# Hybrid diffusion backbone on one core: 67-row products for the grouped-query maximum, four PSUM banks for the gates' projection, rotations one block later

## The chip, the cores and the metric

One core of a Trainium2 chip runs the whole program. The metric is the device time in microseconds (us) of one execution. The engines are named as the profile names them: PE (TensorE, with PEld for its weight loads), DVE (VectorE), ACT (ScalarE), POOL (GpSimd) and SP (SyncE, which issues the DMAs).

## The reference, cut to what matters

Two layers work on 512 latent tokens and 256 context tokens of width 1024. Layer 0 joins chunked gated linear attention (GLA, four heads) with grouped-query attention (GQA, eight query heads of width 64 on two key heads). The change touches the gates of the first and the scores of the second:

```python
def gla_output(o_dirs, og, norm_g):
    o = merge_dirs(o_dirs, 2).transpose(0, 2, 1, 3)
    o = rms_norm(o, norm_g, LN_EPS) * jax.nn.silu(og.reshape(b, n, GLA_HEADS, GLA_DV))

def windowed_gqa(q, k, v, k_ctx, v_ctx, sink):
    s_loc = jnp.einsum('bnqhgd,bnkhd->bhgnqk', qb, kw).astype(F32) * scale
    s_loc = jnp.where(valid, s_loc, -jnp.inf)
    s_ctx = jnp.einsum('bnqhgd,bkhd->bhgnqk', qb, k_ctx).astype(F32) * scale
    p = jax.nn.softmax(jnp.concatenate([s_loc, s_ctx, s_sink], -1), axis=-1)

# in mixer_ab, ahead of it, for the latent tokens alone:
att_lat = windowed_gqa(axial_rope(q_l, row, col), axial_rope(k_l, row, col), v_l, k_c, v_c, sink)
```

Layer 1 (RWKV-7 and latent attention) and the two MLPs are untouched by the change.

## The kernel before, in words

All dense products take three matmuls for one (high by high, high by low, low by high part of fp32 numbers; helper `mm3`, lines 344 to 348). `weights` loads one block of 128x1024 weights by an SP DMA, ACT casts the high part (L323) and DVE subtracts the low part (L324); two buffers of each part, so the cast for block b+2 waits for the end of block b. Every engine runs its own instructions in order. That order is not the order of the source: a list scheduler works it out when the kernel is built, from priorities and its own idea of durations, and the weights of a block come with a raised priority.

The part of layer 0 that the change touches has three stretches.

**Projections and rotation (`mixer0`, the loop at L911).** Block 0 gives the GQA keys (`kg`), blocks 1 to 4 the queries (`qg`). After its 48 wide matmuls ACT moves a block out of PSUM with a factor (L916, L917), PE multiplies it by a permutation (`rp`, L919), and DVE makes the rotation from it (L921 to L923). For the keys ACT then writes the rounded keys `KS` (tile `ks`, L927), DVE the remainders `K2` (tile `k`, L928), and ACT the value one into rows 64 to 66 of `K2` (L929). Two steps of a generator that computes the modulation vectors (DMA `araw`, DVE L392) follow each block. In PSUM this stretch has six banks for products and two for the rest.

**Gates (`mixer0`, the loop at L951).** Four more blocks give the output gates `og`, evicted by ACT (L482 to L484) and DVE (L956). The pool `PB` gives six banks to products and two to tag `u`. Between the blocks runs the set-up of GLA head 0 and its first levels.

**GLA and GQA together (L984 to L989).** A generator `gla` walks over 12 windows (head by pair of chunks); beside the products of one window (`base`, `lev`, `o`) it makes the levels of the next (`lk` on POOL, `lq` on DVE, exponentials on ACT). Two of every five of its steps also advance `gqa`, and what is left of `gqa` runs alone at the end. The pool has two banks each for `b`, `u`, `q` and `qo`. `base` sums matmuls of 128, 64 and 32 columns in one bank and ends with a product of zeros (`zerob`, L655). `gqa` takes the heads in turn: while `attend(h)` runs, `scores(h + 1)` finds the maximum of each query's scores. For it POOL copies the remainders of the queries to `Q2` (tile `q`, two buffers, L737); then there are six products with the context keys (`gsc`, L745 and L746) and four with the latent keys (`gsl`, L753 to L758), each the sum of a 128-row product of `qs` and `KS` and a 64-row product of `Q2[0:64]` and `K2[0:64]`. DVE reduces them (L747, L759). Minus the maximum, in three parts, then goes to rows 64 to 66 of `Q2` (L776), and `attend` uses 67 rows of `Q2` and `K2` (L800, L811), so that the maximum is taken off inside the product. Its masks (L798) and those of the scores (L756) are bf16 products of 128 rows.

Of the kernel before, what the change touches and what calls it, by code (L numbers as in the profile page):

```python
# [7 lines left out]
F32 = mybir.dt.float32  # L8
# [19 lines left out]
PF = dict(b=6, n=2)  # L28
PM = dict(b=4, s=2)
PZ = dict(b=4, n=2, m=2)  # L30
PB = dict(b=6, u=2)
SG = 3
PG = 2, 2, 2, 2
PS = 3, 2, 3
# [223 lines left out]
class Build:  # L258
# [453 lines left out]
    def gqa(self, m0, mx_, queries, KS, K2, vg, hi, lo):  # L712
# [20 lines left out]
        def scores(h):  # L733
            kv, qs = h // 4, QS[h]
            q2[h] = Q2 = m0.tile([99, T], F32R, name="q2", bufs=2)
            for t0, n in PARTS:
                nc.gpsimd.tensor_copy(Q2[0:64, t0:t0 + n], qs[HALF[h % 2], t0:t0 + n])  # L737
            yield
            mx = m0.tile([P, 2, 6], F32, name="mx", bufs=2)
            blk = lambda n: slice(n * P, n * P + P)  # L740
            for i in range(3):
                b = self.bank("gsc", "q").rearrange("p (a k) -> p a k", a=2)
                for a in range(2):
                    q = blk(2 * i + a)
                    mm(b[:, a], qs[:, q], KS[kv][:, CX], start=True, stop=False)  # L745
                    mm(b[:, a], Q2[0:64, q], K2[kv][0:64, CX], start=False, stop=True)  # L746
                nc.vector.tensor_reduce(mx[:, 0, 2 * i:2 * i + 2], b, axis=AX.X, op=ALU.max)  # L747
                yield
            for n in range(4):
                j0, j1 = max(n - 1, 0), min(n + 2, 4)  # L750
                ks = slice(j0 * P, j1 * P)
                b = self.bank("gsl", "q")[:, 0:(j1 - j0) * P]
                mm(b, qs[:, blk(n)], KS[kv][:, ks], start=True, stop=False)  # L753
                for j in (n - 1, n + 1):
                    if 0 <= j < 4:
                        mm(b[:, (j - j0) * P:(j - j0 + 1) * P], self.identb, self.maskb[0 if j < n else 1],  # L756
                           start=False, stop=False)
                mm(b, Q2[0:64, blk(n)], K2[kv][0:64, ks], start=False, stop=True)  # L758
                nc.vector.tensor_reduce(mx[:, 1, n:n + 1], b, axis=AX.X, op=ALU.max)  # L759
                if n % 2:  # L760
                    yield
            ne = m0.tile([P, 6, 2], F32, name="ne", bufs=2)
            nc.vector.tensor_tensor(mx[:, 0, 0:4], mx[:, 0, 0:4], mx[:, 1, 0:4], op=ALU.max)
            nc.vector.tensor_scalar(ne[:, :, 0], mx[:, 0], self.c('sink', h), -1.0, op0=ALU.max, op1=ALU.mult)
            nc.scalar.activation(ne[:, :, 1], ne[:, :, 0], AF.Exp, bias=self.c('sink', h))
            me = mE[h % 2]
            nc.vector.tensor_copy(me[:, :, 0::32], ne)
            nc.vector.tensor_tensor(ne, ne, me[:, :, 0::32], op=ALU.subtract)
            nc.vector.tensor_copy(me[:, :, 1::32], ne)
            nc.vector.tensor_tensor(me[:, :, 2::32], ne, me[:, :, 1::32], op=ALU.subtract)  # L770
            yield
            for t0, n in PARTS:
                b = self.bank("mrow", "q")
                for a in range(n // P):
                    mm(b[0:35, a * P:a * P + P], me[:, t0 // P + a], self.identb, start=True, stop=True)
                nc.scalar.copy(Q2[64:99, t0:t0 + n], b[0:35, :n])  # L776
            yield
# [74 lines left out]
    def mixer0(self):  # L852
# [3 lines left out]
        with tc.tile_pool(name="m0", bufs=1, side="right", reuse_waits="tile") as m0, ExitStack() as m0_, \  # L856
# [25 lines left out]
            with tc.tile_pool(name="ma", bufs=1, reuse_waits="tile") as ma:  # L882
                self.load(ma, 'rope')
                for w in range(2):
                    nc.sync.dma_start(self.sd[w:w + 1], self.scb[0:1, w])

                def mods():
                    for l, j in ((0, 2), (0, 4), (0, 3)):
                        yield from self.ada_chunk(ma, l, j)
                gen = mods()  # L890
                step = lambda n: [next(gen, None) for _ in range(n)]
                nc.vector.memset(a1T, 0.0)

                for t in range(TT):
                    ps = self.bank("a1t", "n")
                    nc.tensor.transpose(ps[0:48, 0:P], at[:, t], ident)
                    nc.scalar.copy(a1T[0:16, t * P:(t + 1) * P], ps[0:16, 0:P])
                    nc.scalar.copy(a1T[32:48, t * P + 1:(t + 1) * P + 1], ps[32:48, 0:P])
                step(3)
                for b in range(4):  # L900
                    w = self.weights(self.a['w0_s'][b].rearrange("p k m -> p (k m)"))
                    for (t0, n), o in zip(PARTS, self.dense(*w, hi, lo, KT)):
                        for hh in range(2):
                            for r in HALF:
                                if b < 2:
                                    nc.scalar.mul(qd[b * 2 + hh][r, t0:t0 + n], o[HALF[hh]], 0.125)
                                else:
                                    nc.scalar.copy(kd[b * 2 - 4 + hh][r, t0:t0 + n], o[HALF[hh]])
                    step(2)

                for b in range(5):  # L911
                    w = self.weights(self.a['w0_s'][4 + b].rearrange("p k m -> p (k m)"))
                    ol, oc = self.dense(*w, hi, lo, KT)
                    x = ma.tile([P, T], F32, name="kg") if b == 0 else qg[b - 1]
                    sc = 1.0 if b == 0 else 0.125
                    nc.scalar.mul(x[:, 0:NL], ol, sc)  # L916
                    nc.scalar.mul(x[:, NL:T], oc, sc)  # L917
                    rp = self.bank("rp", "n")
                    nc.tensor.matmul(rp, self.kr('rperm'), x[:, 0:NL], start=True, stop=True)  # L919
                    rt = ma.tile([P, NL], F32, name="ropet", bufs=2)  # L920
                    nc.vector.tensor_tensor(rt, rp, self.kr('sin'), op=ALU.mult)  # L921
                    nc.vector.tensor_tensor(x[:, 0:NL], x[:, 0:NL], self.kr('cos'), op=ALU.mult)
                    nc.vector.tensor_tensor(x[:, 0:NL], x[:, 0:NL], rt, op=ALU.add)  # L923
                    if b == 0:
                        for i in range(2):
                            for r in HALF:
                                nc.scalar.copy(KS[i][r], x[HALF[i]])  # L927
                            nc.vector.tensor_tensor(K2[i][0:64], x[HALF[i]], KS[i][HALF[i]].bitcast(F32), op=ALU.subtract)  # L928
                            nc.scalar.activation(K2[i][64:67], x[64:67], AF.Identity, scale=0.0, bias=self.c('one')[64:67])  # L929
                    step(2)  # L930
                self.proj_moving(1, hi, lo, ev1)
                step(3)
                for _ in gen:
                    pass
# [27 lines left out]
            mhi, mlo = self.act_tiles()  # L962
            self.psum(PG[0], u=PG[1], q=PG[2], qo=PG[3])
            with tc.tile_pool(name="mb", bufs=1, reuse_waits="tile") as mb:
                self.zerob = mb.tile([32, P], BF16, name="zerob")
                nc.gpsimd.memset(self.zerob, 0.0)
                self.identb = mb.tile([P, P], BF16, name="identb")
                nc.gpsimd.tensor_copy(self.identb, ident)
                self.maskb = [mb.tile([P, P], BF16, name=f"maskb{i}") for i in range(2)]
                mt = m1.tile([P, 2 * P], F32, tag="Dt", name="mt", bufs=4)  # L970
                nc.sync.dma_start(mt, self.a['band'])
                for i in range(2):
                    nc.gpsimd.tensor_copy(self.maskb[i], mt[:, i * P:(i + 1) * P])
                self.gla_setup(mb)

                def queries(i):

                    for r, o, a in ((HALF[0], HALF[1], mhi.k(4 + i)), (HALF[1], HALF[0], mlo.k(4 + i))):
                        for t0, n in PARTS:
                            sl = slice(t0, t0 + n)  # L980
                            nc.scalar.copy(a[r, sl], qg[i][r, sl])
                            nc.vector.tensor_tensor(a[o, sl], qg[i][r, sl], a[r, sl].bitcast(F32), op=ALU.subtract)
                    return mhi.k(4 + i), mlo.k(4 + i)
                att = self.gqa(mb, m0, queries, KS, K2, vg, mhi, mlo)  # L984
                for i, _ in enumerate(self.gla(mb, setup, g, qd, kd, og, mhi, mlo)):
                    if i % 5 < 2:
                        next(att, None)
                for _ in att:
                    pass  # L989
# [1047 lines left out]
```

## Time and profile before

| | us |
|---|---|
| median of 3 runs (2107.3 to 2122.47) | 2110.19 |
| the profiled execution, its own time | 2109.45 |
| its span | 2107.6 |
| PE busy | 1979.7 (94%) |
| DVE busy | 1346.8 (64%) |
| ACT busy | 949.2 (45%) |
| POOL busy | 306.7 (15%) |

Times in the rows are microseconds from the start of the span, durations of one instruction in a group are nanoseconds where the group says so. A matmul's duration is its latency: matmuls overlap, so the distance from one start to the next tells what one costs. The releaser that a row names is the event that came last; where a wait is for several engines it can be another.

### The profile page before, as it was taken

The page shows a single profiled execution, that of the slowest core. Times are in us where ns is not written, and L with a number is a line of the kernel's source. Part 1 is how long each engine was busy: PE and PEld are TensorE (multiplying, and loading weights), DVE is VectorE, ACT ScalarE, POOL GpSimd, SP SyncE. Part 2 cuts the span into 40 slices and gives each one's busy share as a digit, 9 for nine tenths or more (in the row PEclk, how much of TensorE's full clock was granted, in tenths as well). Part 3 has the DMA queues.
Part 4 walks back from the last instruction along what each step waited for, and adds up shares of the span by engine and source line. Part 5 has one row for each costly group of instructions (what it writes and reads, how often), then busy time and mean ns, then how long its engine had stood idle before and what let it go on. Part 6 is the DMA issues. An engine that isn't in the chain of part 4 may idle for free.

```text
span 2107.6 us, 35444 instructions
## 1 busy us (share of the span) xinstructions
PE 1979.7 (94%) x14256; PEld 1636.2 (78%) x14256; DVE 1346.8 (64%) x2471; ACT 949.2 (45%) x1829; POOL 306.7 (15%) x515
## 2 busy tenths in 40 slices
PE   7998999989899999999989999988888899999997
PEld 6877666667788888888877777667677797888887
DVE  8775898737897556534485554568887555444454
ACT  5526676544622222222255646755654544333332
POOL 0003455301200000000021020123342011000001
PEclk9999799999999999999999999988999999999999
DMA  8650000053354555323243100000001412333341
GB/s 294 204 163 14 1 2 1 1 180 103 117 180 136 156 159 148 115 58 98 82 150 120 38 11 13 11 9 2 3 2 33 135 57 86 110 99 90 90 135 41
DMA packets 67049, 181.69 MB, mean 86 GB/s; under 512 B 7490, under 2 KB 12354, under 8 KB 66756
## 3 DMA queue, kind: packets, MB, share of 16 engines
q1 hardware_dynamic: 66884, 179.42, 27.4%
q8 instruction: 112, 1.84, 0.4%
q14 instruction: 53, 0.43, 0.1%
HBM read 172.83 MB, written 5.51 MB: 85 GB/s over the span
## 4 chain that ended last, share of the span: by engine, by line
PE 75%; DVE 14%; ACT 5%; issue 3%; DMA 2%; POOL 1%; DVEq 0%; SPq 0%; ACTq 0%; POOLq 0%
PE mm L346 18%; PE mm L348 18%; PE mm L344 17%; PE var L1054 2%; PE ms L1446 2%; PE go L787 2%; PE gab L1602 1%; PE mo L1472 1%; DMA araw<-in_ada_r_dram 1%; DVE wlo L324 1%; PE lev L661 1%; DVE z L1070 1%; DVE xtmp L1657 1%; DVE X L1660 1%; PE st L1486 1%
## 5 line engine op out<-in xcount | busy, mean ns | idle before, releaser
L323 ACT CAST whi<-wraw 128x1024 fp32r<-128x1024 f32 (+2 forms) x253 | 221.5, 879 | 645.6 <-PE mm L346 559.8
L344 PE MATMUL mm<-acthi,whi 128*128 128x512 f32 (+1 forms) x1464 | 443.6, 349 | 12.3 <-ACT whi L323 11.6
L348 PE MATMUL mm<-acthi,wlo 128*128 128x512 f32 (+1 forms) x1464 | 440.0, 347 | 9.6 <-DVE wlo L324 9.4
L346 PE MATMUL mm<-actlo,whi 128*128 128x512 f32 (+1 forms) x1464 | 442.8, 348 | 2.1 <-POOL actlo L1086 2.0
L324 DVE TENSOR_TENSOR wlo<-wraw,whi 128x1024 fp32r<-128x1024 f32 (+2 forms) x253 | 256.6, 1017 | 221.0 <-ACT whi L323 216.3
L344 PEld LDWEIGHTS mm<-acthi,whi 128*128 128x128 f32 x1464 | 251.4, 192 | 50.7 <-ACT whi L323 14.2
L348 PEld LDWEIGHTS mm<-acthi,wlo 128*128 128x128 f32 x1464 | 252.1, 192 | 49.6 <-DVE wlo L324 13.5
L346 PEld LDWEIGHTS mm<-actlo,whi 128*128 128x128 f32 x1464 | 251.2, 191 | 39.1 <-issue 3.4
L348 PE MATMUL mm<-hh,wlo 128*128 128x512 f32 (+1 forms) x832 | 252.8, 341 | 3.6 <-DVE wlo L324 3.6
L344 PE MATMUL mm<-hh,whi 128*128 128x512 f32 (+1 forms) x832 | 253.8, 343 | 0.2 <-ACT hh L323 0.2
L346 PE MATMUL mm<-hl,whi 128*128 128x512 f32 (+1 forms) x832 | 253.3, 342 | 0.1
L1086 POOL TENSOR_TENSOR actlo<-lnu,acthi 128x256 fp32r<-128x256 f32 (+1 forms) x48 | 60.0, 1265 | 717.7 <-DVE lnu L1084 631.7
L348 PEld LDWEIGHTS mm<-hh,wlo 128*128 128x128 f32 x832 | 143.9, 189 | 23.3 <-DVE wlo L324 4.2
L344 PEld LDWEIGHTS mm<-hh,whi 128*128 128x128 f32 x832 | 143.1, 189 | 20.0 <-issue 1.0
L346 PEld LDWEIGHTS mm<-hl,whi 128*128 128x128 f32 x832 | 143.5, 189 | 19.2 <-issue 0.7
L1158 DVE SCALAR_TENSOR_TENSOR z<-mm,mod,z 128x512 f32<-128x512 f32 (+1 forms) x144 | 94.1, 659 | 95.9 <-PE mm L348 95.7
L392 DVE SCALAR_TENSOR_TENSOR araw<-araw,scb 128x1024 f32<-128x1024 f32 x80 | 97.8, 1223 | 53.8 <-DMA araw<-in_ada_r_dram 52.9
L1012 DVE SCALAR_TENSOR_TENSOR z<-mm,mod,z 128x256 f32<-128x256 f32 (+1 forms) x64 | 34.9, 548 | 79.7 <-PE mm L348 79.2
L323 ACT CAST hh<-relu 128x512 fp32r<-128x512 f32 (+1 forms) x100 | 50.5, 534 | 77.8 <-DVE relu L1110 77.8
L616 POOL TENSOR_TENSOR lk<-kd,Dt 64x128 f32<-64x128 f32 x144 | 74.6, 518 | 48.1 <-ACT Dt L598 19.4
L324 DVE TENSOR_TENSOR hl<-relu,hh 128x512 fp32r<-128x512 f32 (+1 forms) x100 | 56.1, 588 | 26.5 <-ACT hh L323 26.1
L392 DVE SCALAR_TENSOR_TENSOR aprod<-araw,scb 128x1024 bf16<-128x1024 f32 x48 | 58.6, 1222 | 22.4 <-DMA araw<-in_ada_r_dram 22.1
(459 smaller groups left out, 3306.5 us busy)
## 6 DMA issues: line engine op xcount, KB each, us to landing
araw<-in_ada_r_dram SPq DMA_DIRECT2D x80, 512.0 KB, 3.8
wraw<-in_w_dram SPq DMA_DIRECT2D x72, 512.0 KB, 3.6
wraw<-in_w_dram SPq DMA_DIRECT2D x144, 256.0 KB, 2.7
wraw<-in_w_s_dram SPq DMA_DIRECT2D x31, 512.0 KB, 3.7
wraw<-in_w_o_dram SPq DMA_DIRECT2D x22, 512.0 KB, 3.9
scraw<-in_ada_sc_dram SPq DMA_DIRECT2D x8, 512.0 KB, 5.8
shraw<-in_ada_sh_dram SPq DMA_DIRECT2D x8, 512.0 KB, 5.8
x<-in_xT_dram SPq DMA_DIRECT2D x8, 384.0 KB, 5.5
```

The lines of the kernel that those rows point to most:

```text
L323: self.nc.scalar.copy(hi, raw)
L324: (eng or self.nc.vector).tensor_tensor(lo, raw, hi.bitcast(F32), op=ALU.subtract)
L344: mm(o, whi, ahi[:, sl], start=first, stop=False)
L346: mm(o, whi, alo[:, sl], start=False, stop=False)
L348: mm(o, wlo, ahi[:, sl], start=False, stop=last)
L392: self.nc.vector.scalar_tensor_tensor(pr, raw, 1.0, self.scb[:, w], op0=ALU.mult, op1=ALU.mult, accum_out=out(w))
L616: nc.gpsimd.tensor_tensor(K[r, :, x], kk[r, :, x], d[r, :, x], op=ALU.mult)
L787: mm(o, vals(j), p, start=st, stop=False)
L1054: nc.tensor.matmul(var, self.c('o1024', 0, P), sq, start=(k == 0), stop=(k == KT - 1))
L1086: eng.tensor_tensor(lo[:, k, sl], u, hi[:, k, sl].bitcast(F32), op=ALU.subtract)
L1158: nc.vector.scalar_tensor_tensor(z[:, d, sl], o, self.mod[:, l, self.wh(i, parts), 5, d:d + 1], z[:, d, sl], op0=ALU.mult, op1=ALU.add)
L1446: mm(s_[:, j], a[:, c], b[:, j * 384:j * 384 + 384], start=st, stop=sp_)
```

## The change

Three edits. The pool for the gates gets four product banks in place of six. In `scores` the first three spare rows of `Q2` are set to zero by POOL ahead of the copies, and the products of the maximum take all 67 rows of `Q2` and `K2`: the three rows of ones meet three of zeros. `zerob` grows from 32 to 128 rows, so that the product that ends `base` takes 128 rows. In the projections a function `rotate` holds what followed the eviction, and is called for block b-1 after the eviction of block b, and once more after the loop.

```diff
-PB = dict(b=6, u=2)
+PB = dict(b=4, u=2)
...
             q2[h] = Q2 = m0.tile([99, T], F32R, name="q2", bufs=2)
+
+            nc.gpsimd.memset(Q2[64:67].bitcast(F32), 0.0)
             for t0, n in PARTS:
                 nc.gpsimd.tensor_copy(Q2[0:64, t0:t0 + n], qs[HALF[h % 2], t0:t0 + n])
...
-                    mm(b[:, a], Q2[0:64, q], K2[kv][0:64, CX], start=False, stop=True)
+                    mm(b[:, a], Q2[0:67, q], K2[kv][:, CX], start=False, stop=True)
...
-                mm(b, Q2[0:64, blk(n)], K2[kv][0:64, ks], start=False, stop=True)
+                mm(b, Q2[0:67, blk(n)], K2[kv][:, ks], start=False, stop=True)
...
-                for b in range(5):
-                    w = self.weights(self.a['w0_s'][4 + b].rearrange("p k m -> p (k m)"))
-                    ol, oc = self.dense(*w, hi, lo, KT)
-                    x = ma.tile([P, T], F32, name="kg") if b == 0 else qg[b - 1]
-                    sc = 1.0 if b == 0 else 0.125
-                    nc.scalar.mul(x[:, 0:NL], ol, sc)
-                    nc.scalar.mul(x[:, NL:T], oc, sc)
+                def rotate(b, x):
                     rp = self.bank("rp", "n")
...
+                late = None
+                for b in range(5):
+                    w = self.weights(self.a['w0_s'][4 + b].rearrange("p k m -> p (k m)"))
+                    ol, oc = self.dense(*w, hi, lo, KT)
+                    x = ma.tile([P, T], F32, name="kg") if b == 0 else qg[b - 1]
+                    sc = 1.0 if b == 0 else 0.125
+                    nc.scalar.mul(x[:, 0:NL], ol, sc)
+                    nc.scalar.mul(x[:, NL:T], oc, sc)
+                    if late:
+                        rotate(*late)
+                    late = b, x
                     step(2)
+                rotate(*late)
                 self.proj_moving(1, hi, lo, ev1)
...
-                self.zerob = mb.tile([32, P], BF16, name="zerob")
+                self.zerob = mb.tile([P, P], BF16, name="zerob")
```

## Rows read from the trace of the kernel before

**Rows 1.** Busy time by stretch, GLA and GQA: engines, granted clock, DMA.

```profile
200.00:242.00 42.00, 31.34 (x135) 21.42 (x134) 35.58 (x82) 28.31 (x75) 23.97 (x52) 0.59 0.01 4
242.00:270.00 28.00, 27.88 (x173) 18.90 (x172) 22.27 (x71) 18.31 (x56) 12.92 (x28) 1.00 0.01 1
270.00:310.00 40.00, 38.80 (x254) 26.98 (x254) 38.38 (x101) 29.74 (x87) 23.29 (x43) 1.00 0.01 1
310.00:340.00 30.00, 28.28 (x170) 19.31 (x168) 26.97 (x76) 20.31 (x58) 17.71 (x33) 0.94 0.00 1
340.00:400.00 60.00, 59.56 (x391) 41.75 (x390) 49.14 (x140) 37.63 (x124) 34.07 (x65) 1.00 0.00 1
400.00:437.00 37.00, 34.88 (x197) 23.14 (x195) 17.15 (x50) 17.00 (x39) 0.99 (x3) 1.00 0.00 1
```

**Rows 2.** Order of time on PE: 64-row products of `gsc`, and 67-row products of `gst`.

```profile
251.99 0.38 PE L746 MATMUL gsc<-k,q 64*128 64x256 f32 x1
...
252.61 0.38 PE L746 MATMUL gsc<-k,q 64*128 64x256 f32 x1
...
265.62 0.29 PE L811 MATMUL gst<-q,k 67*128 67x256 f32 x1
...
265.87 0.29 PE L811 MATMUL gst<-q,k 67*128 67x256 f32 x1
```

**Rows 3.** Order of time on PE: after a mask, 67 rows, and 64 rows.

```profile
257.96 0.23 PE L798 MATMUL gst<-maskb,identb 128*128 128x128 bf16 x1
258.00 0.36 PE L800 MATMUL gst<-q,k 67*128 67x256 f32 x1
258.19 0.81 PE L787 MATMUL go<-gp,vg 128*128 128x384 f32 x2
...
258.96 0.23 PE L756 MATMUL gsl<-maskb,identb 128*128 128x128 bf16 x1
259.12 0.38 PE L758 MATMUL gsl<-k,q 64*128 64x256 f32 x1
259.43 0.49 PE L651 MATMUL base<-lq,lk 128*128 128x128 f32 x2
```

**Rows 4.** Groups on POOL from 205 to 440 us (busy us, mean ns).

```profile
L494 POOL MEMSET lk<- 128x256 f32 x7 | 2.0, 302 | 0.0
...
L563 POOL MEMSET S<- 64x128 f32 x6 | 1.2, 205 | 6.0 <-PE o L646 5.9
```

**Rows 5.** Order of time on all engines, around the first query block.

```profile
106.17 1.70 ACT L927 CAST ks<-kg 64x768 fp32r<-64x768 f32 x2 [8.20 <-DVE kg L923]
...
112.55 0.60 ACT L916 ACTIVATE qg<-mm 128x512 f32<-128x512 f32 x1
...
113.19 2.07 PE L919 MATMUL rp<-qg,rope 128*128 128x512 f32 x2 [4.60 <-ACT qg L916]
```

**Rows 6.** Busy time by stretch, behind that wait and up to the end of the loop.

```profile
113.20:117.80 4.60, 4.60 (x11) 3.18 (x12) 3.26 (x7) 0.22 (x1) 0.00 (x0) 0.50 0.66 191
...
120.00:145.00 25.00, 25.00 (x136) 20.62 (x135) 22.09 (x39) 4.89 (x9) 0.00 (x0) 1.00 0.60 167
```

**Rows 7.** Order of time on all engines: evictions of the gates, and what follows.

```profile
185.95 1.14 DVE L956 SCALAR_TENSOR_TENSOR og<-mm,col,og 128x512 f32<-128x512 f32 x2 [0.36 <-ACT og L484]
...
191.11 0.88 ACT L482 ACTIVATE og<-mm 128x512 f32<-128x512 f32 x2 [0.39 <-PE mm L348]
...
193.55 1.14 DVE L956 SCALAR_TENSOR_TENSOR og<-mm,col,og 128x512 f32<-128x512 f32 x2 [1.21 <-ACT og L484]
...
207.35 1.14 DVE L956 SCALAR_TENSOR_TENSOR og<-mm,col,og 128x512 f32<-128x512 f32 x2
...
208.24 0.77 PE L651 MATMUL base<-lq,lk 128*128 128x128 f32 x2 [5.97 <-POOL mE L723]
```

**Rows 8.** A short wait of PE in order of time.

```profile
335.23 0.38 PE L745 MATMUL gsc<-ks,acthi 128*128 128x256 f32 x1 [1.01 <-ACT gp L802]
```

**Rows 9.** Busy time of the two microseconds in which the clock falls after it.

```profile
336.00:338.00 2.00, 2.00 (x5) 1.06 (x5) 2.00 (x5) 1.49 (x4) 1.45 (x2) 0.59 0.03 8
```

## The prediction, made before the change was run

> **What bounds the kernel now.** I read the slices of the page first: PE is busy nearly all the time, so only what takes PE's time, or makes it wait, can move the end. Then the busy time by stretch for the stage that the change touches, then the order of time inside it. From 242 to 437 us PE is the bound, but not alone. DVE leaves idle only 28 - 22.27 = 5.7 us from 242 to 270, 40 - 38.38 = 1.6 us from 270 to 310, 3.0 us from 310 to 340, 10.9 us from 340 to 400 and 19.9 us behind 400, where only attention is left [rows 1]. From 200 to 242 the mean granted clock is 0.59, and DVE is idle for 6.4 us of 42 [rows 1]: there PE is slow and DVE nearly full. What an edit saves on PE counts up to what DVE has idle in the same stretch.
>
> **67 rows in place of 64.** It is a PE edit whose price shows in the distance between starts. A pair of 256-column products of 128 and 64 rows repeats every 252.61 - 251.99 = 0.62 us; the same pair with 67 rows in `attend` every 265.87 - 265.62 = 0.25 us [rows 2]. That is 0.37 us for a 64-row product in a run of pairs. After a mask, the 64-row product and its neighbours take 259.43 - 258.96 = 0.47 us from the mask's start to the next start, the 67-row one 258.19 - 257.96 = 0.23 us, so 0.24 us [rows 3]. PE seems to run empty on the way into the smaller shape and out of it; 67 rows are counted as the full shape. Eight heads have six `gsc` products each, in twos, where the first change of shape costs as little as behind a mask: I take 0.33 us of 0.24 to 0.37, so 48 x 0.33 = 15.8 us. The four `gsl` of each head give 32 x 0.24 = 7.7 us. The 24 `zerob` products (12 windows of two chunks) change shape too, but the products ahead of them have 64 and 32 columns, so one change stays: between 0 and 0.24, I take 0.1 us, so 2.4 us. The sum is 26 us of PE time. One head of eight falls before 242 us, so 23 us lie between 242 and 437, or 0.118 us for each microsecond.
>
> Spread evenly, that is 3.3, 4.7, 3.5, 7.1 and 4.4 us for the five stretches. DVE's idle time caps the second at 1.6 and the third at 3.0, which leaves 19.4 us. Not all of that comes through: DVE would be full to 90% or more up to 400 us, and each engine would more often find its input late. I take 0.6 of it, 12 us; ends 6 us (a third) and 23 us (no cap).
>
> The edit adds eight POOL memsets of 3 rows by 768 elements. 256 elements take 302 ns and 128 take 205 ns [rows 4]; on that line 768 take 0.69 us, together 5.5 us. POOL is busy 34.07 of 60 us and less elsewhere [rows 1], and the memset waits for the same buffer as the copies behind it. Behind it on POOL stand those copies and the `lk` products of the next GLA window, made one window ahead; their cover is POOL's idle time. I take nothing; without the cover 5.5 us. The three more rows of the moving and loaded operands cost nothing that rows 2 would not hold. The copy of the maxima into the same rows gets a further writer to wait for, but it already waits for products that come later.
>
> **Rotations a block later.** The keys' rotation is late on DVE, ACT stands 8.20 us for it, then makes `KS` and the ones, and so moves the first query block out of PSUM only at 112.55; its rotation product on PE waits 4.60 us for that [rows 5]. Behind the wait PE runs 4.60 us at a granted clock of 0.50, the 1.2 GHz level [rows 6], so half of it, 2.3 us, is lost besides. Together 6.9 us at one place; I found no other wait of PE of such a kind in the loop. With the edit the query block's eviction comes ahead of the keys' copies on ACT, and PE takes up the rotation of a block one block of products later, when its input is long there. Moved with the matmul are three DVE operations of each block, and the keys' four ACT copies, two ACT fills and two DVE subtractions. Next late could be the cast of the weights two blocks on, behind those copies on ACT, or DVE: it is busy 22.09 of 25 us after the stall [rows 6], and the 6.9 us in which it could catch up are gone. The generator's DMAs keep their place in the source behind each block, on SP's queue. I take 6 us, ends 1 and 7.
>
> **Four banks for the gates.** It seems a loss: products can run one block less ahead. But a block needs two banks, and with four the fourth block needs those of the second, which DVE has emptied by 185.95 + 1.14 = 187.1, while the third block ends only about 191.1, where ACT begins on it [rows 7]. So 4 us cover it; the third block by the same pattern has more. If the cover went, PE would wait for the rest. What it gives is at the end. The first `base` of GLA starts at 208.24, and the row names POOL, with 5.97 us of waiting; but that memset has no part in `base`, and DVE's first eviction of the last gate block (207.35, two in 1.14 us) ends just before [rows 7]. I read it as a wait for the bank: with six banks four blocks wrap around to the first two, and the next pool's `b` is laid on these. With four, these hold the third block, emptied from 193.55 on [rows 7]. So `base` can begin 6 us earlier, on the heels of the last gate block, and PE may keep its clock. In exchange the bank of `z` (tag `u`) then comes under the last block. But DVE has only 6.4 us idle up to 242. I take 4 us, ends 0 and 6.
>
> **Sum.** 12 + 6 + 4 = 22 us. The profiled execution took 2109.45 us, 0.7 us under the median of the runs, which is nothing here. 2109.45 - 22 = 2087.5 us, 1.1% below the median.
>
> **Rivals.** First, DVE takes nearly all: it is the bound in the stage by then, 4 us come from the 67 rows (the tail alone), 1 us from the banks, 6 us from the rotation: 2109.45 - 11 = 2098.5. For it speak the 38.38 of 40 us [rows 1]; against it, that DVE's idle time also lies before 270 and behind 340.
>
> Second, rows don't count, and the 0.62 us of rows 2 come from something else in `gsc`, such as its operands: then only 6 + 4 us come, 2099.5 us. Rows 3 speak against it, where neighbours differ and the gap is still there. The Trainium skill has both sides. "TensorE: Matmul & The Clock Gate", in "Why this matters for your kernels", says that a single product of 32 rows takes as long as one of 128, and by that the 67 rows would give nothing; "TensorEngine Tiling (Array Packing)", under "Key Properties", says that a change of the tiling mode drains the engine, and by that the sum above stands. The trace agrees with the second.
>
> Third, and slower: the clock. PE fell to 0.59 in the two microseconds after a wait of only 1.01 us [rows 8, 9], with DVE the bound there. A faster PE waits more between 270 and 340, where DVE is full. PE has 38.80 + 28.28 = 67.1 us busy there [rows 1], less 8.2 saved 58.9; all at the lower level they need 117.8 us in place of 70, 48 us more. With the other gains, 22 less 0.6 x 4.6, that gives 2109.45 + 48 - 19 = 2138 us. It turns the result from where about half of these 70 us run at 1.2 GHz: 58.9 x 1.5 - 70 = 18 us, which eats the 19. Against it: waits of that length are rare now, and a slow PE soon catches up with DVE's queue and stops waiting.
>
> **How the numbers follow.** My forecast (all three act, in the sizes above) has 0.62, DVE takes nearly all 0.20, rows don't count 0.08, the clock 0.10. The forecast's own ends are 2109.45 - 23 - 7 - 6 = 2073 and 2109.45 - 6 - 1 = 2102; the order on every engine is worked out anew, which can add or take some microseconds on both sides. The range that holds 8 in 10 reaches from 2068 to 2105 and takes in the first two rivals. A measurement tells about 1% from no change, 21 us, so the line lies at 2089, just above the forecast: of the 0.62, I give 0.48 to below it (it has more room below, if the clock holds from 202 us on), and 0.02 of the rivals; slower by over 1% is most of the clock rival, 0.08; the rest 0.42.
>
> **What would show it.** Pairs of `gsc` 0.25 us apart, and `zerob` followed at once; no `rp` that waits for `qg`, and no stretch at 0.50 behind it; the first `base` at the heels of the last gate block (its distance from there, not the absolute time); from 270 to 340 DVE at 95% or more, with the waits of PE now for DVE's tiles. Wrong I would be if the early stretch keeps the full clock and its queues close up (a larger gain), if the recomputed order puts the keys' copies ahead of a weight cast and PE waits there, or if DVE's 1.6 us of idle time from 270 to 310 hold the whole stage back.

## The result, and the profile after

The changed kernel takes 2087.05 us (median of 4 runs, 2082.48 to 2089.79) beside 2111.19 us for the kernel before on the same chip (4 runs, 2107.3 to 2122.47). The ratio is 0.9884, 95% interval 0.9859 to 0.9909: 1.2% faster. 2087.5 us was predicted. The profiled execution took 2088.43 us, with a span of 2086.6 us against 2107.6 us. The total fits; its terms do not all fit, and the experiments below are about these.

All line numbers in this part are those of the changed kernel, unless the kernel before is named.

**Rotations.** Order of time on PE at the first query block, which stood still for 4.60 us before [rows 5]:

```profile
113.39 0.51 PE L348 MATMUL mm<-acthi,wlo 128*128 128x512 f32 x2
113.74 1.02 PE L915 MATMUL rp<-qg,rope 128*128 128x512 f32 x2
114.20 0.92 PE L344 MATMUL mm<-acthi,whi 128*128 128x512 f32 x2
```

Busy time by stretch around it, and up to the end of the loop:

```profile
105.00:120.00 15.00, 15.00 (x82) 12.45 (x82) 13.10 (x25) 6.86 (x10) 0.00 (x0) 1.00 0.54 164
120.00:145.00 25.00, 25.00 (x141) 21.72 (x140) 23.66 (x40) 5.20 (x10) 0.00 (x0) 1.00 0.58 173
```

`rp` carries no wait in square brackets any more (2.94 to 4.85 us in the six traces without this edit), and the stretch at 0.50 [rows 6] is gone. The first of the last gate block's two evictions on ACT starts at 199.24 us, in the kernel before at 204.64: 5.4 us earlier. Forecast: 6. (Executions of kernels that don't differ up to that place differ there by up to 2 us.)

**Four banks.** Order of time on PE at the start of GLA:

```profile
196.29 0.51 PE L348 MATMUL mm<-acthi,wlo 128*128 128x512 f32 x2
196.64 0.39 PE L651 MATMUL base<-lq,lk 128*128 128x128 f32 x2
...
199.16 0.23 PE L655 MATMUL base<-zerob 128*128 128x128 bf16 x1 [1.67 <-POOL zerob L974]
202.91 2.93 PE L508 MATMUL z<-a1T,con 48*128 48x512 f32 x4 [3.52 <-DVE og L964]
206.52 0.58 PE L747 MATMUL gsc<-ks,acthi 128*128 128x256 f32 x1 [0.69 <-DVE acthi L990]
208.04 0.58 PE L748 MATMUL gsc<-k,q 67*128 67x256 f32 x1 [0.94 <-POOL q L739]
```

`base` starts at the heels of the last gate block, as forecast, and its wait of 5.97 us [rows 7] is gone. But the four waits behind it add up to 1.67 + 3.52 + 0.69 + 0.94 = 6.82 us. The first product of `ms` (L674), the end of the first window, starts 6.2 us earlier, of which 5.4 were there before GLA began; first the changed kernel, then the kernel before:

```profile
227.14 1.22 PE L674 MATMUL ms<-sq,con 128*128 128x256 f32 x2 [0.54 <-ACT sq L672]
```

```profile
233.35 1.22 PE L674 MATMUL ms<-sq,con 128*128 128x256 f32 x2 [0.35 <-ACT sq L672]
```

The other 0.8 us are not the banks' alone, for the first head's 67-row products lie in them too. From that eviction on ACT to `ms` it is 27.90 us here, 28.71 in the kernel before, and 28.16 in the run below that has the rows and six banks: about 0.3 us for the banks. Forecast: 4. And the banks cost something at another place, the first block of the gates, where PE didn't wait before:

```profile
158.78 0.39 PE L344 MATMUL mm<-acthi,whi 128*128 128x256 f32 x1 [1.25 <-ACT vt L880]
```

This wait of 1.25 us, for the eviction of the projection ahead of the gates (`vt`), stands in the traces of all five versions with four banks and in none of the nine with six.

**67 rows.** Order of time on PE in a run of pairs, which took 0.62 us a pair before [rows 2], and the chain of one chunk's small products:

```profile
246.37 0.28 PE L748 MATMUL gsc<-k,q 67*128 67x256 f32 x1
246.49 0.28 PE L747 MATMUL gsc<-ks,actlo 128*128 128x256 f32 x1
246.60 0.28 PE L748 MATMUL gsc<-k,q 67*128 67x256 f32 x1
246.72 0.39 PE L651 MATMUL base<-lq,lk 128*128 128x128 f32 x2
247.04 0.53 PE L654 MATMUL base<-lq,lk 128*64 128x64 f32 x12
247.50 0.23 PE L655 MATMUL base<-zerob 128*128 128x128 bf16 x1
247.57 1.11 PE L661 MATMUL lev<-lq,lk 128*128 128x128 f32 x8
```

A pair now repeats every 246.60 - 246.37 = 0.23 us, and `zerob` is followed after 0.07 us. Busy time in three stretches that hold about the same work as 242 to 270, 270 to 340 and 340 to 437 us before [rows 1] (VectorE executes 72, 173 and 190 instructions in them, before 71, 177 and 190, as the rows count them):

```profile
235.00:260.00 25.00, 24.31 (x172) 17.56 (x171) 23.25 (x72) 18.73 (x57) 14.13 (x30) 1.00 0.00 1
260.00:326.00 66.00, 60.57 (x425) 43.98 (x426) 64.50 (x173) 50.27 (x145) 41.51 (x76) 0.97 0.01 1
326.00:413.00 87.00, 82.00 (x583) 60.59 (x583) 66.29 (x190) 54.11 (x160) 37.74 (x71) 1.00 0.00 1
```

The stretch as a whole has shrunk from 195 to 178 us. VectorE's work in it is the same, 23.25 + 64.50 + 66.29 = 154.0 us (before 153.9, from [rows 1]); PE's busy time fell from 189.4 to 166.9, by 22.5 us. So 17 of the 22.5 us taken from PE came out at the end. The last products of the attention (`goc`) start 24.1 us earlier; first the changed kernel, then the kernel before:

```profile
415.83 1.13 PE L789 MATMUL goc<-gp,vg 128*128 128x256 f32 x4
```

```profile
439.97 1.13 PE L787 MATMUL goc<-gp,vg 128*128 128x256 f32 x4
```

24.1 less the 6.2 above are 17.9 us for the rows behind the first window. Forecast: 12.

**What is late now.** One of the ten-microsecond stretches of 260 to 340 us, in each of which VectorE is busy for 95% or more, and the wait of PE that stands in it:

```profile
320.00:330.00 10.00, 8.33 (x54) 6.63 (x55) 9.94 (x20) 8.46 (x24) 7.66 (x11) 0.83 0.00 0
```

```profile
321.67 0.39 PE L747 MATMUL gsc<-ks,acthi 128*128 128x256 f32 x1 [1.93 <-ACT gp L804]
```

This is the wait of [rows 8], grown from 1.01 to 1.93 us, with the fall of the clock behind it [rows 9]. The memsets on GpSimd, one group:

```profile
L737 POOL MEMSET q<- x8: 732/732/732, 203.4 to 386.3; 3x768 f32 x8
```

They take 0.73 us each (estimate: 0.69), and nothing is recorded as waiting for them directly. But the first one, at 203.4, stands on POOL ahead of the `lk` products, and VectorE's wait for these has grown; first the changed kernel, then the kernel before:

```profile
205.19 0.43 DVE L597 TENSOR_TENSOR Dt<-ld 128x256 f32<-128x256 f32 x1 [1.94 <-POOL lk L616]
```

```profile
209.15 0.43 DVE L597 TENSOR_TENSOR Dt<-ld 128x256 f32<-128x256 f32 x1 [0.66 <-POOL lk L616]
```

With the rows and their memsets alone this wait is 1.54 us, with the rotations alone 0.65.

Behind the attention the stages are the same in both kernels, and the lead shrinks from 24.1 to 21.0 us at the end of the span. Such differences come between executions of one kernel: the runs above spread over 7 and 15 us.

### The profile page after: what moved, and what is told of

Read it like the earlier page. It is cut to its first block, busy times and chain, and to the rows that moved or that the text cites. A ratio compares the mean times of both kernels' runs of the same rounds, so it can differ in the third digit from the quotient of the medians.

```text
span 2086.6 us, 35456 instructions
## 1 busy us (share of the span) xinstructions
PE 1951.6 (94%) x14256; PEld 1626.4 (78%) x14256; DVE 1345.9 (64%) x2471; ACT 950.4 (46%) x1829; POOL 312.9 (15%) x523
## 4 chain that ended last, share of the span: by engine, by line
PE 72%; DVE 17%; ACT 5%; issue 3%; DMA 2%; SPq 0%; POOL 0%; DVEq 0%; ACTq 0%; POOLq 0%
PE mm L346 18%; PE mm L348 18%; PE mm L344 18%; PE var L1062 2%; PE ms L1454 2%; PE mo L1480 1%; PE gab L1610 1%; DVE z L1078 1%; DVE xtmp L1665 1%; DVE X L1668 1%; DMA araw<-in_ada_r_dram 1%; PE go L789 1%; DVE wlo L324 1%; PE st L1494 1%; DVE R L1780 1%
## 5 line engine op out<-in xcount | busy, mean ns | idle before, releaser
L324 DVE TENSOR_TENSOR wlo<-wraw,whi 128x1024 fp32r<-128x1024 f32 (+2 forms) x253 | 257.2, 1020 | 215.1 <-ACT whi L323 210.6
L324 DVE TENSOR_TENSOR hl<-relu,hh 128x512 fp32r<-128x512 f32 (+1 forms) x100 | 56.2, 588 | 26.6 <-ACT hh L323 26.2
```

What stands on the lines that cost most here:

```text
L324: (eng or self.nc.vector).tensor_tensor(lo, raw, hi.bitcast(F32), op=ALU.subtract)
```

## Experiments

The kernel before ran beside each group of four: 2112.22 us for the first, 2113.44 for the second, 2111.69 for the third. All ratios are to it, with 95% intervals.

### One edit at a time

**The 67-row products and the memset alone.**

```
+nc.gpsimd.memset(Q2[64:67].bitcast(F32), 0.0)
...
-mm(b[:, a], Q2[0:64, q], K2[kv][0:64, CX], start=False, stop=True)
+mm(b[:, a], Q2[0:67, q], K2[kv][:, CX], start=False, stop=True)
...
-mm(b, Q2[0:64, blk(n)], K2[kv][0:64, ks], start=False, stop=True)
+mm(b, Q2[0:67, blk(n)], K2[kv][:, ks], start=False, stop=True)
```

> The kernel before with the 67-row products and their memset alone (zerob, banks and rotation as before). Theory (each 64-row product makes PE change shape twice): the stretch of GLA and GQA gets shorter by 15 to 17 us, pairs of gsc follow each other 0.25 us apart, the first base still waits until the last gate eviction, so a time of about 2094. Rival (rows don't count): below 3 us, 2107 or more. Rival (DVE holds the stage): 4 to 8 us, 2102 to 2106.

2089.7 us, ratio 0.9896 (0.9863 to 0.9928): 22.0 us. The rows are nearly the whole result, and more than the 12 us that I gave them in the prediction and the 15 to 17 us ahead of this run. But for the eight memsets every engine executes the instructions of the kernel before in the same order, so a new order is not what gained them.

**The rotations alone.** The loop of the change with `rotate` and `late`, everything else as before.

> The kernel before with the rotations a block later alone. Theory: the 4.6 us wait of PE and the half-speed stretch behind it are gone, and the gates' evictions come 5.4 us earlier, as in the changed kernel; all of it reaches the end: about 2105. Rival (the later stage has slack for it, because DVE bounds it): 0 to 2 us, 2108 or more.

2105.92 us, ratio 0.9973 (0.9955 to 0.9991): 5.7 us (1.9 to 9.5), and the wait of `rp` is gone. As forecast. In exchange a projection behind the loop (`mv`, L474) waits 1.02 us for weights from DVE (`wlo`, L324).

**Four banks alone.**

```
-PB = dict(b=6, u=2)
+PB = dict(b=4, u=2)
```

> The kernel before with four banks for the gates alone. Theory after the result: the first base starts 6 us earlier, but z takes over the wait for the last gate eviction, so 0 to 1 us: about 2110. Rival (as predicted): 4 us, 2106. Rival (gates run into each other): slower by 1 us or more, with PE waiting for og in the gates.

2117.96 us, ratio 1.0023 (1.0005 to 1.0041): no gain, a small loss. Its waits of PE from 190 to 240 us, totals by line:

```profile
PE o L645 <- DVE A L663: 4.3, 1, 4.3
PE z L508 <- DVE og L956: 3.3, 1, 3.3
PE base L655 <- POOL zerob L966: 1.7, 1, 1.7
PE gsc L746 <- POOL q L737: 1.1, 1, 1.1
```

The wait of 5.97 us [rows 7] comes back as 3.3 + 1.7 + 1.1 = 6.1 us, and the 1.25 us for `vt` at the start of the gates are added. The order is that of the kernel before on every engine. The rest of the loss goes together with a lower clock: the mean granted clock of the span is 0.9598 over these 12 executions and 0.9626 over the 29 of the kernel before beside them. Within these 29 an execution is about 1.7 us longer for each 0.001 less (a straight line through them), so 0.0028 go with about 4.6 us (estimate). Why the clock is lower, no run shows.

**128 zero rows alone.**

```
-self.zerob = mb.tile([32, P], BF16, name="zerob")
+self.zerob = mb.tile([P, P], BF16, name="zerob")
```

> The kernel before with zerob of 128 rows alone. Theory: 24 products, 0.1 us each at most, 0 to 2.4 us: about 2109. Rival (both changes of shape count): 4 to 6 us, 2105.

2113.44 us, ratio 1.0002 (0.9983 to 1.0022): nothing that can be measured. On PE the step is there: from the start of L654 to the start of `lev` one chunk takes 256.14 - 255.61 = 0.53 us, in the kernel before 256.84 - 256.22 = 0.62 us, so 0.09 us for each of 24, about the 0.1 that I took.

The four parts sum to -22.0 - 5.7 + 4.9 + 0.4 = -22.4 us beside the change's -24.1 (medians); they add up within the intervals.

### Is it the switch between row counts, or the 64 rows?

In the kernel before, the two 64-row products of a pair of blocks stand side by side: 128, 64, 64, 128 rows.

```
-mm(b[:, a], qs[:, q], KS[kv][:, CX], start=True, stop=False)
-mm(b[:, a], Q2[0:64, q], K2[kv][0:64, CX], start=False, stop=True)
+ops = ((qs[:, q], KS[kv][:, CX]), (Q2[0:64, q], K2[kv][0:64, CX]))
+for s, (x, y) in enumerate(ops[::-1] if a else ops):
+    mm(b[:, a], x, y, start=s == 0, stop=s == 1)
```

> The kernel before with the two 64-row products of a pair of query blocks side by side (128, 64, 64, 128 rows in place of 128, 64, 128, 64): as many products of 64 rows as before, half as many switches between row counts. Theory (it is the switch that costs, not the 64 rows): the second 64-row product starts 0.12 us behind the first, the pair takes 0.3 us less, 24 pairs save 8 us of TensorE and 4 to 7 us of time: 2104 to 2107 us. Rival (a product of 64 rows is slow in itself): nothing is saved, 2110 to 2113 us.

2106.45 us, ratio 0.9965 (0.9948 to 0.9982): 7.4 us gained, with as many 64-row products as before. Order of time on PE:

```profile
250.46 0.36 PE L747 MATMUL gsc<-ks,actlo 128*128 128x256 f32 x1
250.75 0.50 PE L747 MATMUL gsc<-k,q 64*128 64x256 f32 x2
251.18 0.39 PE L747 MATMUL gsc<-ks,actlo 128*128 128x256 f32 x1
251.41 0.34 PE L795 MATMUL gst<-acthi,ks 128*128 128x384 f32 x1
```

Four products take 251.41 - 250.46 = 0.95 us here, 2 x 0.62 = 1.24 us in the kernel before [rows 2] and 2 x 0.23 = 0.46 us with 67 rows. One island of 64-row products costs (1.24 - 0.46) / 2 = 0.39 us over full shape; doubling its size adds only 0.95 - 0.46 - 0.39 = 0.10 us. So it is the switch that costs, by this trace. The Trainium skill, "TensorEngine Tiling (Array Packing)", "Key Properties", says that a change of the tiling mode drains the engine; the trace agrees and gives 0.39 us as the price of going there and back.

### Why four banks gave so little

**Six banks in the changed kernel** (`PB` back to `b=6`), with the same order of instructions on every engine:

> The changed kernel with six banks for the gates' projection as before: the other three edits stay. The order of instructions on every engine is that of the changed kernel. Theory (the step forecast at 4 us gained under 1 us, because the product of z then waits for the last gate's eviction in place of base): base waits 5 to 6 us again, z waits for nothing, and the time is 2086 to 2089 us, 0 to 2 us over the changed kernel. Rival A (four banks are worth what was forecast when the other edits stand beside them): 2090 to 2092 us. Rival B (they cost in company too, as they cost alone): 2081 to 2084 us.

2085.43 us, ratio 0.9870 (0.9842 to 0.9898), beside 0.9884 for the change. `base` waits again, those of `z`, `zerob` and `gsc` are gone, and so is the one for `vt` (waits of PE from 190 to 240 us):

```profile
PE o L645 <- DVE A L663: 7.1, 1, 7.1
PE base L651 <- DVE og L964: 6.2, 1, 6.2
```

**A bank of its own for the last gate block**: the products of this block get a tag with two banks, so neither `base` nor `z` lies under it.

```
-PB = dict(b=4, u=2)
+PB = dict(b=4, u=2, x=2)
...
-for (t0, n), o in zip(PARTS, self.dense(*w, hi, lo, KT)):
+for (t0, n), o in zip(PARTS, self.dense(*w, hi, lo, KT, tag="x" if b == 3 else "b")):
```

> The changed kernel with the last gate block's product in two banks of its own beside the four, so that neither base nor z comes under a bank that this block still holds. Theory (VectorE and GpSimd are full from the last gate block on, so a product that starts sooner only waits elsewhere): the wait of z of 3.5 us goes, the wait for the zeroed rows or for the half query takes over within 10 us, and the time is 2085 to 2087.5 us, at most 2 us below the changed kernel. Rival (the moved wait of z is what ate the forecast gain): the first maskings start 3 to 4 us earlier and the time is 2083 to 2084 us.

2089.94 us, ratio 0.9892 (0.9872 to 0.9911): nothing gained. The order is again the same, and the wait for `vt` is still there. Waits of PE in the same stretch:

```profile
PE o L645 <- DVE A L663: 6.9, 1, 6.9
PE gsc L747 <- DVE acthi L990: 5.5, 1, 5.5
PE base L655 <- POOL zerob L974: 1.6, 1, 1.6
PE gsc L748 <- POOL q L739: 0.9, 1, 0.9
```

What none of the three moves is the work of the other engines. Order of time on VectorE, the last eviction of the gates and the first selection of the levels, first in the changed kernel, then with six banks, then with the bank of its own:

```profile
202.10 1.14 DVE L964 SCALAR_TENSOR_TENSOR og<-mm,col,og 128x512 f32<-128x512 f32 x2
...
212.21 0.96 DVE L663 COPY_PREDICATED A<-con,lev 128x128 f32<-128x128 uint32 x3
```

```profile
203.67 1.14 DVE L964 SCALAR_TENSOR_TENSOR og<-mm,col,og 128x512 f32<-128x512 f32 x2
...
213.76 0.96 DVE L663 COPY_PREDICATED A<-con,lev 128x128 f32<-128x128 uint32 x3
```

```profile
205.07 1.14 DVE L964 SCALAR_TENSOR_TENSOR og<-mm,col,og 128x512 f32<-128x512 f32 x2
...
215.16 0.96 DVE L663 COPY_PREDICATED A<-con,lev 128x128 f32<-128x128 uint32 x3
```

The distance is 10.11, 10.09 and 10.09 us, whether `base` starts 5.46 us ahead of that eviction (196.64), 5.39 us ahead (199.68) or 0.89 us behind it (204.56). Between the two VectorE waits once for GpSimd (the 1.94 us above; 1.93 in each of the two other kernels) and then works off its queue without a pause, through the first selection, which carries no wait, to the end of the window. Busy time of that stretch in the changed kernel, and the wait of PE for the selections that come last in it:

```profile
205.19:228.40 23.21, 12.40 (x62) 9.26 (x60) 22.62 (x51) 14.78 (x39) 13.69 (x25) 0.65 0.00 1
```

```profile
224.28 0.80 PE L645 MATMUL o<-A,vt 128*128 128x128 f32 x2 [8.30 <-DVE A L663]
```

VectorE is busy 22.62 of 23.21 us. ACT is full too up to the first selection (8.77 of the 8.90 us from the last eviction's end to it, in all three kernels), but later stands 6.39 us for VectorE. The queue of VectorE has the same length behind the last gate block's eviction in all three, and doesn't ask when `base` started. A product that starts earlier only waits longer for a selection: 8.3 us in the changed kernel, 7.1 with six banks. No run here shortens this queue, so that it decides is read from the traces and not tested by an edit.

### More of the same: the other narrow products

The selection of the sink takes 99 rows, 96 of them zero, instead of 3, and `z` takes 128 rows instead of 48.

```
-sl = sel[sink, 64 - 64 * par:192 - 64 * par]
-mm(ob, sl, Q2[sink, 0:NL], start=False, stop=True)
+sl = sel[:, 64 - 64 * par:192 - 64 * par]
+mm(ob, sl, Q2[:, 0:NL], start=False, stop=True)
...
```

> The changed kernel with the remaining narrow products of this stage made full: the selection of the sink takes 99 rows (96 of them zero) instead of 3, and z takes 128 rows instead of 48. Theory (each switch of TensorE to fewer rows and back costs 0.2 to 0.33 us, and VectorE sets the pace for about half of the stage): 16 selections and 8 products of z, about 24 switches by 0.28 us are 6.7 us of TensorE, of which 2 to 5 us show: 2082 to 2085 us. Rival (the selections stand in time that VectorE sets, or 3 rows at the far end of the array switch at no cost): 2086 to 2088 us.

2089.81 us, ratio 0.9887 (0.9866 to 0.9907): nothing, where I expected 2 to 5 us. PE does save: from the products of `U` ahead of one selection to the `lev` behind it 283.00 - 281.59 = 1.41 us became 1.13. But the stage does not get shorter in the profiled execution, the longest of six (2084.82 to 2092.57 us). Busy time of the stretch that corresponds to 235 to 413 us of the changed kernel:

```profile
239.00:419.00 180.00, 164.29 (x1163) 123.84 (x1162) 153.40 (x427) 121.02 (x355) 92.33 (x173) 0.96 0.00 1
```

PE is busy 2.6 us less (166.9), idle 15.7 us instead of 11.1, and the mean clock is 0.96 instead of 0.99. What was true of the first 22.5 us is not seen for the next; whether for want of idle time on VectorE or for the clock of this execution, the run doesn't tell.

### Does VectorE set the pace?

The reduction of `gsl` is taken twice, once in the changed kernel and once in the kernel before; this adds 32 instructions of 0.48 us, 15.4 us by their durations. VectorE's busy time over the whole span rises less, by 10.1 us in the changed kernel (1345.9 to 1356.0) and by 6.4 in the kernel before (1346.8 to 1353.2).

```
-nc.vector.tensor_reduce(mx[:, 1, n:n + 1], b, axis=AX.X, op=ALU.max)
+for _ in range(2): nc.vector.tensor_reduce(mx[:, 1, n:n + 1], b, axis=AX.X, op=ALU.max)
```

> The changed kernel with the second maximum of each head (the reduction of gsl on VectorE) taken twice, with the same result: 32 instructions of 0.48 us more, 15.4 us of VectorE and nothing else. Theory (the saved time of TensorE has made VectorE the bound of the stretch, 24 us of idle time left in 178): most of it shows, 9 to 15 us, so 2096 to 2102 us. Rival (TensorE still sets the pace there): 2 to 6 us, 2089 to 2093 us.

> The kernel before with the same reduction taken twice, 15.4 us more of VectorE. Theory (VectorE has 41 us of idle time in 195 there and TensorE sets the pace): 2 to 8 us show, 2113 to 2119 us, clearly less than the same edit costs in the changed kernel. Rival (VectorE was the bound already, and the rows gained in another way): 10 to 15 us, 2121 to 2126 us.

In the changed kernel 2105.61 us, ratio 0.9968 (0.9949 to 0.9988): 18 us more than the change, by the ratios, and above the 2096 to 2102 us expected. In the kernel before 2125.65 us, ratio 1.0081 (1.0055 to 1.0108): 17 us more. My theory wanted a clearly smaller loss in the kernel before and fell on that; the time lies in the rival's range. Both losses are larger than what VectorE's busy time rose by. The order of the stage is worked out anew in both, which is part of the price. Busy time of the stretches that correspond to 235 to 413 us of the change and to 242 to 437 us of the kernel before:

```profile
240.00:433.00 193.00, 175.78 (x1184) 127.38 (x1184) 164.76 (x466) 124.11 (x361) 91.42 (x174) 0.96 0.00 1
```

```profile
242.00:457.00 215.00, 201.60 (x1200) 136.74 (x1200) 162.13 (x466) 126.81 (x365) 86.05 (x172) 0.96 0.01 3
```

They have grown by 15 and 20 us, with PE busy 8.9 and 12.2 us longer although it has no more to do: the mean clock fell from 0.99 to 0.96. The rest is waiting, 6.1 and 7.8 us.

**Work off VectorE**, both with six banks: one more level of the decays' differences on GpSimd (12 x 0.64 us), and the multiplication with the output gate on GpSimd (12 x 0.48 us).

```
-DTP = 32, 16
+DTP = 32, 16, 8
```

> The changed kernel with six banks for the gates (the variant measured last) and one more of the differences of the decay levels (the level of 8) on GpSimd in place of VectorE: 12 instructions of 0.64 us leave VectorE, 7.7 us over the stage. Theory (VectorE is the bound from 260 to 390 us, GpSimd has a third of its time idle): 2 to 6 us gained on 2085.4 us, so 2079 to 2083 us. Rival (GpSimd's products are as late as VectorE's, so the wait only moves): 2084 to 2089 us.

```
-nc.vector.tensor_tensor(rs, rs, og[:, h, sl], op=ALU.mult)
+nc.gpsimd.tensor_tensor(rs, rs, og[:, h, sl], op=ALU.mult)
```

> The changed kernel with six banks for the gates and the multiplication of each window's normalized output with the output gate on GpSimd in place of VectorE: 12 instructions of 0.48 us leave VectorE, 5.7 us over the stage; no other product waits for its result before the projection behind the stage. Theory (VectorE is the bound): 1 to 5 us gained on 2085.4 us, so 2080 to 2084 us. Rival (nothing moves, or GpSimd's later products come later): 2085 to 2089 us.

2093.95 us, ratio 0.9921 (0.9893 to 0.9948), and 2093.06 us, ratio 0.9922 (0.9899 to 0.9946): both some 8 us above the 2085.43 us that they start from, and above what either theory gave. Against the changed kernel itself their intervals overlap. Neither took load off VectorE: its busy time over the span is 1346.4 and 1349.0 us, with six banks 1346.5, for its other instructions took longer. So these two runs do not test what less work on VectorE is worth. Nor does the clock explain both: over all six executions its mean is 0.9643 and 0.9668, with six banks 0.9655. Both have an order of their own.

So "VectorE is the bound" is neither shown nor refuted: adding to it costs more than was added, and nothing here took from it.

No version here is measurably faster than the changed kernel; with six banks it is as fast.

## Why the prediction was right, and where its terms were not

**The rotations** went as written: 5.4 us in the trace and 5.7 in the run of their own, for 6. What I named as next late, the weights two blocks on, does come late in most executions: `mv` waits 0.38 to 1.98 us for `wlo` in six of the eight traces with the new loop, not in the changed kernel's own. ACT still stands 8.0 us for the keys' rotation, off PE's path.

**The 67 rows: the price held, the share did not.** I priced 23 us of PE time in the stretch; PE's busy time fell by 22.5. I capped the gain by VectorE's idle time in each part at 19.4 us; the three stretches shrank by 28 - 25 = 3, 70 - 66 = 4 and 97 - 87 = 10 us, where the caps were 3.3, 4.6 and 11.5, so each gave about nine tenths of its cap (the boundaries are matched to about 1 us). The step that failed is "I take 0.6 of it": the share was 17 / 19.4 = 0.88. My reason for 0.6, that each engine would more often find its input late, had an effect of 2 us, not of 7. The rule that the gain ends where VectorE's idle time ends is tested by the middle stretch alone, where PE's busy time fell by 67.1 - 60.6 = 6.5 us and 4 came out; in the two others the cap was PE's own saving. It fits there, and the doubled reduction speaks against it as a general rule: in the kernel before VectorE had 41 us idle, and the load cost 17 us all the same.

**The memsets.** I took nothing for them, with POOL's idle time as cover and POOL "busy 34.07 of 60 us and less elsewhere". By share that isn't so (23.29 of 40 and 17.71 of 30 are more), and the first memset found no cover: VectorE's wait for `lk` grew from 0.66 to 1.94 us. What that was worth at the end, no run shows.

**Four banks: the event came, its worth did not.** The term of 4 us was mis-sized: about 0.3 us at the start of GLA, less 1.25 us at the start of the gates, and no gain in the comparison with six banks. The cover of 4 us that I worked out is that of the later blocks; I did not ask what the first block's banks lie under. For the gain I had named both reasons against it, that `z` comes under the last block and that VectorE has little idle time there, and still took 4 of the 6 us. The experiments tell them apart: without the wait of `z` nothing is gained either. By the traces it is VectorE's queue that decides, busy 22.62 of 23.21 us behind the last gates.

**Luck in the sum.** The two errors, some 6 us too little for the rows and 4 to 5 too much for the banks, nearly cancel; 3 us of the lead went in the stages behind. That the total came within 0.5 us of the forecast is luck, where the spread of the runs alone is 7 us.

**The rivals.** That rows don't count is out: 22 us come from them alone. The Trainium skill, "TensorE: Matmul & The Clock Gate", "Why this matters for your kernels", says that one product of 32 rows takes as long as one of 128. For a 64-row product among its like the trace agrees (0.10 us for the second in an island, where 0.12 lie between starts at full shape); the sentence says nothing of the switch. That VectorE takes nearly all had the right mechanism and the wrong size: VectorE's idle time was enough for 17 us. The fall of the clock happens once between 260 and 340 us, and costs PE 10 x (1 - 0.83) = 1.7 us.

**What stays open.** Why the clock is lower with four banks alone, with the order of every engine unchanged; why a doubled reduction costs as much in the kernel before, where VectorE has 41 us of idle time in 195, and in both more than VectorE's busy time grew. The traces show longer stretches at the lower clock in these runs, but not what would have happened without them.

## What to carry over

A product with fewer rows among full ones costs PE the switch there and back, here 0.39 us, more than the product itself; fill it with zero rows, or put the narrow ones side by side. What such a saving is worth can be estimated stretch by stretch, with the idle time of the next busiest engine as a cap; here nine tenths came out, though loading that engine cost more than the same view allows. Before giving a product an earlier start, follow the chain to the next engine that is full: if its queue has a fixed length from an event that does not move, the earlier start is worth next to nothing. And when a pool of banks gets smaller, look at the first product in it as well as at the last: here it waited 1.25 us that the prediction had not priced.

## What was not expected of the hardware

The same short wait of PE is followed by very different stretches at the lower clock in two executions of one order. The kernel with 128 zero rows alone has the order of the kernel before, and waits 1.06 us where that one waits 1.01 [rows 8]:

```profile
337.20 0.38 PE L745 MATMUL gsc<-ks,acthi 128*128 128x256 f32 x1 [1.06 <-ACT gp L802]
```

The kernel before then falls to 0.59 for two microseconds [rows 9], stands at 0.56 for the next two and holds 1.00 from 340 to 400 [rows 1]. This one runs at 0.50, the 1.2 GHz level, for all of the next stretch, with PE busy throughout:

```profile
340.00:350.00 10.00, 10.00 (x31) 6.74 (x30) 6.00 (x11) 5.08 (x17) 5.67 (x9) 0.50 0.00 0
350.00:360.00 10.00, 10.00 (x73) 7.68 (x73) 7.80 (x28) 4.13 (x13) 1.84 (x5) 0.86 0.00 0
```

That is 10 x 0.50 + 10 x 0.14 = 6.4 us of PE's time lost behind one wait of 1 us, where the kernel before lost 2 x 0.41 + 2 x 0.44 = 1.7 us, and as much as the rotations' edit is worth. That the wait brings it on is not shown, only that it stands ahead of it in both. One profiled execution therefore does not tell an edit of that size; the medians of runs do.
